# Layer 1's query panels: made ahead of the attention jobs, or beside them, two pairs ahead

## The chip, the cores and the metric

The kernel runs on one core of one Trainium2 chip. The metric is the time of one execution in device microseconds; what counts is the median of several runs. The engines are named as the profile names them: PE (TensorE, matrix products; PEld is its loading of weights), DVE (VectorE), ACT (ScalarE), POOL (GpSimd) and SP (SyncE, which here only issues DMAs).

## What is computed

Two layers of a diffusion backbone over 512 latent tokens and 256 context tokens, model width 1024, all in 32-bit floats. Layer 0 mixes latent attention and neighbourhood attention, layer 1 is sliding-window attention with 16 query heads over 2 key heads. Each layer ends in a SwiGLU block, and the result is a normalized latent stream. The part around the change is layer 1's attention. Cut to that part, the reference reads:

```python
def odd_mixer(a_lat, a_ctx, rows, cols, w_in, sinks, w_out, ctx_out):
    q, k, v = split(a_lat @ w_in, s)          # 16 query heads, 2 key and 2 value heads of 64
    q = axial_rope(q, rows, cols)
    k = axial_rope(k, rows, cols)
    qc, kc, vc = split(a_ctx @ w_in, n_ctx)
    o_lat, o_ctx = swa_heads(q, k, v, qc, kc, vc, sinks, ctx_out)
    return o_lat @ w_out, (o_ctx @ w_out if ctx_out else None)

# in swa_heads, for each block of 128 queries: scores on the 256 context keys and on the
# keys of its own block and the neighbours, a sink logit beside them, one softmax
    s_ctx = einsum(qg, kc) * scale
    s_lat = where(band_ok, einsum(qg, kb) * scale, NEG_INF)
    p = softmax(concatenate([sink, s_ctx, s_lat]))
    o = einsum(p[ctx part], vc) + einsum(p[lat part], vb)
```

## The kernel before

**Layout.** Activations are kept features by tokens. A model vector of 1024 features is eight tiles of 128 partitions. `A` (line 1545) is the modulated input of layer 1: eight pairs of tiles, each a high part and a low part, since a product of two 32-bit floats is made of three products (high by high, high by low, low by high: lines 317, 319 and 320). The 16 heads are worked as eight pairs, each pair 128 features.

**A query panel.** `swa_queries(p)` (lines 1581 to 1584) makes the queries of pair p. `load_w` (lines 301 to 308) loads 512 KB of weights by SP into a tile `wr`, ACT casts the high part `wh` (line 306), and DVE subtracts for the low part `wl` (line 307). There are three buffers of each. `project` (line 742) then runs eight times three products of 512 columns into one PSUM bank of the kind d, and yields after each three: eight steps. Behind the last, `rope` (line 443) turns the result: ACT copies it out (line 447), DVE shuffles (448), POOL multiplies twice and adds (450 to 452). `put_q` (line 687) writes it for the two heads: ACT casts each head's 64 rows (694) and DVE subtracts the low half (695).

**A job.** `swa_jobs` (line 1623) yields two jobs a pair, each with both heads and two blocks of 128 queries: 16 jobs. A job computes scores on PE (728 and 729: for each head and block two products over 256 context keys and two over 256 or 384 latent keys), adds masks and takes the running minimum on DVE (538), takes exponentials on ACT (534), transposes the 128 by 128 blocks of the weights on PE in groups of up to four (482; 18 blocks a job), copies each group out of PSUM on DVE or ACT (473, 474), and sums the values by them on PE (528). ACT copies the sum out (612). After a pair's second job `swa_finish` divides by the denominators (four transposes, 349, and a product on DVE, 465).

**Order.** `attend` (line 652) writes a job's scores between the transposes and the weighted sum of the job ahead of it, by a pattern of letters: f a step of the new job, b one of the old job, s a place for side work. There are four s in this stage's pattern (`PATTERN`, line 67). Side work is a queue of generators (`beside`, line 939). `step` (line 634) takes one step of the first generator in the queue, and a generator that ends runs its rest within the next call. `STEPS[2]` (line 72), put into `rate` at line 1642, says how many such steps are shared out over the four places of a job.

The program's text is not the final order. The tile framework traces it, gives each instruction a priority by its place in the text, and a scheduler then fixes each engine's order by priority among what is ready in a simulated timeline (`SCHED`, line 63). Larger numbers are later. `shifted` (line 627) adds to the priority of what is traced in it, and `lower[0]` is what `step` adds to side work: 150 by default (`LOWER`), 50 (`LQ`) for the query panels here. Each engine then executes its list strictly in order.

**The stage.** After the keys, the values and panel 0 (lines 1586 to 1607), panels 1 to 7 are put into side work and drained (lines 1633 to 1640), all before the first job is traced. Then come the jobs. During them the only side work is one `swa_finish` a pair, one step. After the jobs the residual `H`, which was parked in DRAM, is loaded back (1645 to 1649), the outputs are split into high and low (1650; 343, 344), and the output projection runs with `w_out1` (1652; the residual is added at 1238).

**Buffers.** The tag b has 24 tiles: `A` takes 16 until its last product; values, `k32`, `v32`, each rope's x, y and result, each pair's output, and later the residual take the others. The tag st has 12: four for the keys, two for each pair's queries, later the outputs' high parts. PSUM has eight banks: three of kind s (scores), two t, two d, one o. The groups of transposes alternate between t and d (`TURN`, line 64); the query panels take d (`PQ`, line 327).

Of the kernel before, what the change touches and what calls it, by code (L numbers as in the profile page):

```python
# [30 lines left out]
LATS = slice(0, NL)  # L31
# [14 lines left out]
LAG = 1  # L46
EV = "dr"
QF = 0
LQ, EACH = 50, 0
NR = "nb"  # L50
PE_MODS = ((0, 1), (0, 0), (0, 5))
KEEP = 1
# [12 lines left out]
LOWER = 150  # L65
# [3 lines left out]
LATE = ((0, 1, 3, 5, 7), ()), (0,) * 4 + (1, 2, 2, 2, 1, 2, 2, 2, 1, 2, 3, 2, 1, 2, 3, 2, 0, 0), ((2,), (2,)) + ((0, 2, 4, 6),) * 3  # L69
FIRST = 2000  # L70
SUMS = 5, 6
STEPS = ((2, 3, 4, 4), 5, 3)
HALVES = (slice(0, 256), slice(256, 512))
SWAP8 = [(i // 16) * 16 + (i % 16 + 8) % 16 for i in range(32)]
SWAP16 = [(i + 16) % 32 for i in range(32)]
# [23 lines left out]
def hybrid_kernel(ctx: ExitStack, tc, I, out):  # L99
# [6 lines left out]
    def T(tag, shape, dt=F32):  # L106
        count[0] += 1
        if tag not in SIZES:
            return sb.tile(shape, dt, tag=tag, name=f"{tag}_{count[0]}", bufs=BUFS.get(tag, 1))
        n = int(np.prod(shape[1:]))  # L110
        t = sb.tile([P, SIZES[tag] // (2 if dt == mybir.dt.bfloat16 else 4)], dt, tag=tag, name=f"{tag}_{count[0]}",
                    bufs=BUFS[tag])[: shape[0], :n]
        if len(shape) == 3:
            t = t.rearrange("p (a b) -> p a b", a=shape[1])
        return t

    def B(dt=F32, tag="b"):
        return T(tag, [P, NT], dt)
# [12 lines left out]
    V, S, G, PE = nc.vector, nc.scalar, nc.gpsimd, nc.tensor  # L131
# [4 lines left out]
    def f(ap):  # L136
        return ap.bitcast(F32) if ap.dtype == F32R else ap
# [3 lines left out]
    def behind(ins, *before):  # L141

        for x in before:
            tc.add_manual_dep(ins.ins, x.ins.name, mybir.DependencyInfo(mybir.DependencyClass.NoSync,
                              mybir.DependencyReason.DATA), reason="products in one run")
        return ins
# [479 lines left out]
    @contextmanager  # L626
    def shifted(by):
        tc.cur_priority += by
        yield
        tc.cur_priority -= by  # L630

    side_work, lower = deque(), [LOWER]

    def step(n=1):

        for _ in range(n):
            while side_work:
                try:
                    with shifted(lower[0]):
                        next(side_work[0])  # L640
                    break
                except StopIteration:
                    side_work.popleft()

    def drain(gen=None):

        while side_work and (gen is None or gen in side_work):
            step()
# [32 lines left out]
    def new_q(tag="st"):  # L681
        return [B(F32R, tag) for _ in range(2)]

    def new_k(tag="st"):
        return [(B(F32R, tag), B(F32R, tag)) for _ in range(2)]

    def put_q(ts, scale, hi=None, lo=None, after=()):


        def use(src, c):  # L690
            for side, t in enumerate(ts):
                r, x = slice(64 * side, 64 * side + 64), slice(64 - 64 * side, 128 - 64 * side)
                if scale is None:
                    behind((hi or S.copy)(t[r, c], src[r]), *after)
                    (lo or G.tensor_tensor)(t[x, c], src[r], f(t[r, c]), op=ALU.subtract)
                    continue
                S.activation(t[r, c], src[r], AF.Copy, scale=scale)
                V.scalar_tensor_tensor(t[x, c], src[r], scale, f(t[r, c]), op0=ALU.mult, op1=ALU.subtract)

        return use  # L700
# [24 lines left out]
    def stacked_scores(t1, ks):  # L725
        def scores(o, q, keys):
            x = t1[:, q * P : (q + 1) * P]
            PE.matmul(o, x, ks[0][:, keys], start=True, stop=False)
            PE.matmul(o, x, ks[1][:, keys], start=False, stop=True)

        return scores
# [10 lines left out]
    def project(src, use, cols=(LATS, CTXS), m=P, every=2, eng=None, w=None, get=PQ):  # L742

        w = w or load_w(src, KT, m, eng)
        for c in cols:
            o, _ = banks([c], get, m)[0]
            for k in range(KT):
                mm3([(o, c)], (w[0][:, k : k + 1], w[1][:, k : k + 1]), A[k : k + 1], k == 0, k == KT - 1)
                if k % every == every - 1:
                    yield  # L750
            use(o, c)
# [184 lines left out]
    sets = [(new_q(), new_k()) for _ in range(2)]  # L936
    for t in range(6):
        started[:] = put_vs(VN, t, ov[t])
    def beside(gen):
        side_work.append(gen)  # L940
        return gen
# [11 lines left out]
    def put_rope(t, tabs, swap, rows=P, scale=1.0, tag="b", eng=None):  # L953
        def use(src, c):
            if c is LATS:
                rope(t[:rows, c], src, tabs, swap, scale, tag, eng)
            else:
                S.activation(t[:rows, c], src, AF.Copy, scale=scale)

        return use  # L960
# [68 lines left out]
    def split_pair(p):  # L1029

        tag = ("b", "st")[p - 2]
        q, k = raws[2 * p - 4 : 2 * p - 2]
        sets.append((new_q(tag), new_k(tag)))
        up, dn = slice(0, 64), slice(64, 128)
        t0, t1 = sets[p][0]
        S.copy(t0[:, :NT], q)
        lo = q.bitcast(F32R)
        V.tensor_tensor(lo, q, f(t0[:, :NT]), op=ALU.subtract)
        yield
        dma(t1[up, :NT], t0[dn, :NT])  # L1040
        dma(t1[dn, :NT], lo[dn])
        dma(t0[dn, :NT], lo[up])
        (h0, l0), (h1, l1) = sets[p][1]
        S.copy(h0[:, :NT], k)
        V.tensor_tensor(l0[:, :NT], k, f(h0[:, :NT]), op=ALU.subtract)
        yield
        for x, y in ((h0, h1), (l0, l1)):
            dma(y[up, :NT], x[dn, :NT])
            dma(y[dn, :NT], x[dn, :NT])
            dma(x[dn, :NT], x[up, :NT])  # L1050
        yield
# [63 lines left out]
    def latent_operands(h):  # L1115
        p, s = divmod(h, 2)
        r, u = NOPE[s], USED[s]
        rr = slice(32 * (h % 4), 32 * (h % 4) + 32)
        if p < 2:
            if p == 0:  # L1120
                KA.append([T("st", [P, NT], F32R) for _ in range(2)])
            QA[s].append([T("st", [P, NT], F32R) for _ in range(2)])
            for t in [*(KA[s] if p == 0 else ()), *QA[s][p]] if s else ():
                (V if "z" in EV else G).memset(f(t[:32]), 0.0)
            if p == 0:
                for i in range(2):
                    dma(KA[s][i][ROPE[s]], KR[i][:32])
        (ka, kc), (qa, qb) = KA[s], QA[s][p % 2]
        for x, (hi, lo) in ((kn[p], (ka, kc)), (qn[p], (qa, qb))):
            S.copy(hi[r], x[r])  # L1130
            (V if "l" in EV and p < 1 else G).tensor_tensor(lo[r], x[r], f(hi[r]), op=ALU.subtract)
        for t, x in zip((qa, qb), QR[h // 4]):
            if "d" in EV:
                dma(t[ROPE[s]], x[rr])
            else:
                G.dma_start(t[ROPE[s]], x[rr])

        def scores(o, q, keys):
            q = slice(q * P, (q + 1) * P)
            PE.matmul(o, qa[u, q], ka[u, keys], start=True, stop=False)  # L1140
            PE.matmul(o, qb[u, q], ka[u, keys], start=False, stop=False)
            PE.matmul(o, qa[u, q], kc[u, keys], start=False, stop=True)

        return scores
# [12 lines left out]
    def na_jobs():  # L1157
        for p in range(4):
            if p == 3:
                lower[0] = L3  # L1160
            for x in ORDER[p]:
                beside(split_pair(int(x)) if x in "23" else {"n": latent_norms, "m": mla_prepare}[x]())
            rate[0] = STEPS[0][p], BG[p]
            if p % 2 == 0:
# [33 lines left out]
    def mla_jobs():  # L1198
        phase[0], lower[0] = 1, LOWER
        rate[0] = STEPS[1], BG[4]  # L1200
        ready.append(latent_operands(1))
# [342 lines left out]
    new = []  # L1544
# [34 lines left out]
    sets = {}  # L1579

    def swa_queries(p, every=1, get=PQ):
        q, sets[p] = B(), new_q()
        yield from project(I["w_in1"][p], put_rope(q, rope1, SWAP16, scale=0.125), (LATS,), every=every, get=get)
        put_q(sets[p], None, lo=V.tensor_tensor)(q[:, LATS], LATS)

    k32, v32, KS = B(), B(), new_k()
    kv_use = put_rope(k32, rope1, SWAP16), put(v32)
# [34 lines left out]

    def swa_jobs():
        for p in range(8):
            kv = p // 4
            po = B()
            sums, mins = T("sm", [P, 6, 2]), T("sm", [P, 6, 2])
            hs = [Head(s, stacked_scores(sets[p][s], KS[kv]), keys_of(VS, kv), span, swa_bias,
                       sink_neg[:, 2 * p + s : 2 * p + s + 1], sums, mins) for s in range(2)]
            yield from pair_jobs(hs, po, False, swa_finish(p, po, sums, mins))  # L1630
            OS.append(po)

    phase[0] = 2
    lower[0] = LQ
    for p in range(1, 8):
        beside(swa_queries(p))
        if EACH:
            drain()
            lower[0] += EACH
    drain()  # L1640
    lower[0] = LOWER
    rate[0] = STEPS[2], 0
    attend(swa_jobs())
    drain()
    H = []
# [184 lines left out]
```

## Time and profile before

| what | us |
|---|---|
| runs before, median of 3 | 1558.71 |
| lowest and highest of the 3 | 1557.58, 1560.64 |
| the profiled execution, its time | 1558.19 |
| the profiled execution, its span from first to last instruction | 1556.3 |

The page of the profile shows one execution. Busy times are sums for each engine; an instruction's row has its line, its engine, its output and inputs by the program's names (buffer numbers left out: `psd` is any bank of kind d), its shape and count. A number in brackets or behind a bar is idle time of the engine just before, with what ended it. A matmul's length is modelled and overlaps the next one, so what PE has to spend on one is read from the distance between two starts. The chain of the profile is followed back from the last instruction, at each step to what released it; its rows have a start and the time that counted. The windows give busy times between two moments, counted from the start of the span.

### The profile page before, as it was taken

Reading aid. Unit: us, or ns where it says so; the run is one execution under the profiler, and the core shown is the slowest. Engines: PE = TensorE matmul, PEld = TensorE weight load, DVE = VectorE, ACT = ScalarE, POOL = GpSimd, SP = SyncE. Lnnn points to the kernel's source line nnn. Section 1 sums busy time; section 2 is a strip of 40 time slices with the busy share of each in tenths; the row PEclk is TensorE's granted clock in tenths of the full one; section 3 lists DMA queues with packets and bytes.
Section 4 is the critical chain, followed back from the end, with each engine's and each line's share of the span. In section 5 each row is a group of like instructions: output and inputs, shape, how many; then the busy total and the mean of one; then the engine's idle time right before and its main releaser. Section 6 shows DMA issues by size and latency. Waiting matters only on the chain.

```text
span 1556.3 us, 26589 instructions
## 1 busy us (share of the span) xinstructions
PE 1529.0 (98%) x10048; PEld 1374.9 (88%) x10048; DVE 1176.5 (76%) x2408; ACT 768.0 (49%) x1531; POOL 217.0 (14%) x269
## 2 busy tenths in 40 slices
PE   9999999999999999999999999999999999999998
PEld 8788877877999898999999988877789899899998
DVE  4799867676868687777768676789967779678685
ACT  4532677674555242432424335457856455354453
POOL 0021043110101102012021122470012000000001
PEclk9999999999999999999999999999999999999999
DMA  9674632013634545537465494110214223323222
GB/s 321 249 226 142 161 125 65 11 63 138 227 128 139 206 134 182 205 118 288 142 249 187 150 358 139 55 41 1 90 57 167 63 91 126 107 84 131 88 94 89
DMA packets 79073, 219.39 MB, mean 141 GB/s; under 512 B 10720, under 2 KB 17888, under 8 KB 78944
## 3 DMA queue, kind: packets, MB, share of 16 engines
q1 hardware_dynamic: 61280, 147.42, 28.6%
q0 software_dynamic: 16512, 68.69, 12.4%
q8 instruction: 79, 1.29, 0.3%
q10 hardware_dynamic: 1152, 1.57, 0.3%
q14 instruction: 50, 0.41, 0.1%
HBM read 186.97 MB, written 23.07 MB: 135 GB/s over the span
## 4 chain that ended last, share of the span: by engine, by line
PE 88%; DVE 7%; ACT 2%; issue 2%; DMA 1%; POOL 0%; DVEq 0%; ACTq 0%; POOLq 0%
PE pss L1401 5%; PE pss L1400 5%; PE pss L1399 5%; PE pso L528 5%; PE pss L320 4%; PE pss L317 4%; PE pss L319 4%; PE psd L317 4%; PE psd L320 4%; PE psd L319 4%; PE pst L317 3%; PE pst L320 3%; PE pst L319 3%; PE pst L1401 3%; PE pst L1399 3%; PE pst L1400 3%
## 5 line engine op out<-in xcount | busy, mean ns | idle before, releaser
L306 ACT CAST wh<-wr 128x1024 fp32r<-128x1024 f32 (+2 forms) x148 | 115.5, 795 | 224.2 <-DMA wr<-in_w_dn_dram 35.0
L307 DVE TENSOR_TENSOR wl<-wr,wh 128x1024 fp32r<-128x1024 f32 (+2 forms) x145 | 130.9, 910 | 80.6 <-ACT wh L306 76.3
L534 ACT ACTIVATE p<-p,sm 128x512 f32<-128x512 f32 (+3 forms) x144 | 105.0, 730 | 25.8 <-DVE sm L538 25.2
L1399 PE MATMUL pss<-b,wh 128*128 128x384 f32 (+1 forms) x346 | 107.7, 312 | 0.5 <-ACT b L343 0.5
L1400 PE MATMUL pss<-b,wh 128*128 128x384 f32 (+1 forms) x346 | 107.8, 312 | 0.0
L1401 PE MATMUL pss<-b,wl 128*128 128x384 f32 (+1 forms) x346 | 107.0, 311 | 0.0
L319 PE MATMUL psd<-b,wh 128*128 128x512 f32 (+2 forms) x254 | 88.6, 349 | 0.0
L273 DVE CUSTOM_DVE_ANT_0 p<-rope,cond 128x1024 bf16<-128x1024 f32 x64 | 76.8, 1219 | 11.4 <-DMA rope<-in_mod_w_dram 11.2
L317 PE MATMUL psd<-b,wh 128*128 128x512 f32 (+2 forms) x214 | 79.1, 370 | 2.8 <-ACT pl L474 2.2
L528 PE MATMUL pso<-ph,b 128*64 128x256 f32 (+1 forms) x384 | 77.9, 362 | 1.0 <-DVE ph L473 0.9
L528 PE MATMUL pso<-pl,b 128*64 128x256 f32 (+1 forms) x384 | 78.4, 363 | 0.0
L320 PE MATMUL psd<-b,wl 128*128 128x512 f32 (+2 forms) x214 | 77.5, 363 | 0.0
L1401 PE MATMUL pst<-b,wl 128*128 128x384 f32 (+1 forms) x226 | 70.6, 313 | 1.5 <-DVE wl L1387 1.5
L1386 ACT CAST wh<-pl 128x512 fp32r<-128x512 f32 x78 | 44.9, 619 | 53.6 <-PE pss L1400 22.7
L1399 PE MATMUL pst<-b,wh 128*128 128x384 f32 (+1 forms) x226 | 70.7, 313 | 0.6 <-ACT p L1449 0.6
L263 POOL DMA_DIRECT2D rope<-in_mod_w_dram x48 | 25.6, 533 | 323.0 <-DVE mod L273 312.1
L1400 PE MATMUL pst<-b,wh 128*128 128x384 f32 (+1 forms) x226 | 70.5, 312 | 0.0
L1386 ACT CAST wh<-wr 128x1024 fp32r<-128x1024 f32 x39 | 41.0, 1051 | 57.7 <-PE pst L1400 14.8
L319 PE MATMUL pss<-b,wh 128*128 128x256 f32 (+3 forms) x216 | 68.4, 316 | 0.0
L317 PE MATMUL pss<-st,wh 128*128 128x512 f32 (+2 forms) x198 | 67.5, 341 | 0.3 <-ACT wh L306 0.3
L320 PE MATMUL pss<-st,wl 128*128 128x512 f32 (+2 forms) x198 | 67.5, 341 | 0.1
L1399 PEld LDWEIGHTS pss<-b,wh 128*128 128x128 f32 x346 | 65.0, 188 | 1.1 <-ACT b L343 0.8
(606 smaller groups left out, 5290.7 us busy)
## 6 DMA issues: line engine op xcount, KB each, us to landing
wr<-in_w_gu_dram SPq DMA_DIRECT2D x88, 512.0 KB, 4.1
rope<-in_mod_w_dram POOLq DMA_DIRECT2D x48, 512.0 KB, 3.9
wr<-in_w_dn_dram SPq DMA_DIRECT2D x73, 256.0 KB, 2.9
wr<-in_w_out_dram SPq DMA_DIRECT2D x32, 512.0 KB, 3.9
p<-home POOLq DMA_DIRECT2D x40, 384.0 KB, 5.6
home<-p POOLq DMA_DIRECT2D x40, 384.0 KB, 5.9
wr<-in_w_in_dram SPq DMA_DIRECT2D x21, 512.0 KB, 3.9
ph<-in_mod_w_dram SPq DMA_DIRECT2D x24, 256.0 KB, 2.8
```

What stands on the lines that cost most here:

```text
L273: behind(V.tensor_tensor_reduce(out=T("p", [P, D], mybir.dt.bfloat16), in0=w, in1=cond[:, v, :], op0=ALU.mult, op1=ALU.add, scale=1.0, sca ...
L306: behind(S.copy(h, r), *after[:1])
L307: behind((G if eng else V).tensor_tensor(lo, r, f(h), op=ALU.subtract), *after[1:])
L317: ins = PE.matmul(o, wh[:, k], mh[:, c], start=first and k == 0, stop=False)
L319: PE.matmul(o, wh[:, k], ml[:, c], start=False, stop=False)
L320: PE.matmul(o, wl[:, k], mh[:, c], start=False, stop=last and k == n - 1)
L528: ins = PE.matmul(o[64 * i : 64 * i + 64, c], v(kt), t, start=n == 0, stop=n == len(moving[i]) - 1)
L534: S.activation(p[:, c], p[:, c], AF.Exp, bias=nm, scale=-1.0, accum_out=dn)
L1386: S.copy(h, t)
L1399: PE.matmul(o, wh, xh, start=first and k == 0, stop=False, skip_group_check=not first)
L1400: PE.matmul(o, wh, xl, start=False, stop=False, skip_group_check=not first)
L1401: PE.matmul(o, wl, xh, start=False, stop=k == 3, skip_group_check=not first)
```

## The change

Panels 2 to 7 are no longer drained ahead of the jobs. Panel 1 alone is. At the beginning of pair p, for p below 6, the generator of panel p + 2 is put into the side work, and it is stepped at the places of the jobs, with five steps a job instead of three and the default of 150 added to the priority in place of 50. A pair's two jobs thus have ten steps, for the eight of a panel, in whose wake the rope and `put_q` are traced, and the one of the finish. `sets[p]` is now set when a panel is complete, and a pair whose panel is not complete steps the side work until it is.

```diff
@@ -46,7 +46,6 @@
 LAG = 1
 EV = "dr"
 QF = 0
-LQ, EACH = 50, 0
 NR = "nb"
 PE_MODS = ((0, 1), (0, 0), (0, 5))
 KEEP = 1
@@ -69,7 +68,7 @@
 FIRST = 2000
 SUMS = 5, 6
-STEPS = ((2, 3, 4, 4), 5, 3)
+STEPS = ((2, 3, 4, 4), 5, 5)
 HALVES = (slice(0, 256), slice(256, 512))
@@ -1579,9 +1578,10 @@
     sets = {}
 
     def swa_queries(p, every=1, get=PQ):
-        q, sets[p] = B(), new_q()
+        q, new = B(), new_q()
         yield from project(I["w_in1"][p], put_rope(q, rope1, SWAP16, scale=0.125), (LATS,), every=every, get=get)
-        put_q(sets[p], None, lo=V.tensor_tensor)(q[:, LATS], LATS)
+        put_q(new, None, lo=V.tensor_tensor)(q[:, LATS], LATS)
+        sets[p] = new
 
@@ -1622,6 +1622,10 @@
 
     def swa_jobs():
         for p in range(8):
+            while p not in sets:
+                step()
+            if p < 6:
+                beside(swa_queries(p + 2))
             kv = p // 4
             po = B()
             sums, mins = T("sm", [P, 6, 2]), T("sm", [P, 6, 2])
@@ -1631,14 +1635,8 @@
             OS.append(po)
 
     phase[0] = 2
-    lower[0] = LQ
-    for p in range(1, 8):
-        beside(swa_queries(p))
-        if EACH:
-            drain()
-            lower[0] += EACH
+    beside(swa_queries(1))
     drain()
-    lower[0] = LOWER
     rate[0] = STEPS[2], 0
     attend(swa_jobs())
     drain()
```

## The prediction

> **What bounds the kernel now.** I read the page first, then the stretch of layer 1's queries and attention by windows, then its PE timeline, its chain, its waits and its groups. The page says that there is little to win anywhere on PE:
>
> ```profile
> span 1556.3 us, 26589 instructions
> PE 1529.0 (98%) x10048; PEld 1374.9 (88%) x10048; DVE 1176.5 (76%) x2408; ACT 768.0 (49%) x1531; POOL 217.0 (14%) x269
> ```
>
> The change touches one stretch. The windows below (us, then busy time of PE, PEld, DVE, ACT, POOL, granted clock, DMA) split it where the first weighted sum of the attention (L528) starts:
>
> ```profile
> 985.00:1042.70 57.70, 56.16 (x291) 46.62 (x289) 46.84 (x83) 31.56 (x53) 45.59 (x29) 1.00 0.21 64
> 1042.70:1147.00 104.30, 102.83 (x840) 81.98 (x839) 95.06 (x315) 80.59 (x196) 0.00 (x0) 1.00 0.10 37
> ```
>
> Before 1042.7 PE makes all query panels while POOL turns them (45.6 us busy). After it PE and DVE are both nearly full and POOL does nothing. PE at 102.8 of 104.3 is a modelled figure, so I check it by starts. Rows of the PE timeline (start, us, what) give what one matmul takes from PE when PE is fed:
>
> ```profile
> 1011.30 0.28 PE L728 MATMUL pss<-st,st 128*128 128x256 f32 x1
> 1011.42 0.28 PE L729 MATMUL pss<-st,st 128*128 128x256 f32 x1
> 1011.78 0.39 PE L317 MATMUL psd<-b,wh 128*128 128x512 f32 x1
> ...
> 1017.14 0.39 PE L320 MATMUL psd<-b,wl 128*128 128x512 f32 x1
> 1017.37 0.28 PE L728 MATMUL pss<-st,st 128*128 128x256 f32 x1
> ...
> 1017.61 0.34 PE L728 MATMUL pss<-st,st 128*128 128x384 f32 x1
> 1017.79 0.33 PE L729 MATMUL pss<-st,st 128*128 128x384 f32 x1
> ...
> 1018.44 0.50 PE L317 MATMUL psd<-b,wh 128*128 128x512 f32 x1 [0.32 <-ACT b L447]
> ```
>
> A panel is the 24 matmuls from 1011.78 to 1017.37: 5.6 us, 0.233 each. A score matmul takes 0.12 (256 columns) or 0.18 (384). The chain has four transposes in 0.44 us and a job's weighted sum in 2.10:
>
> ```profile
> 1036.33 0.44 PE psd L482 x4
> ...
> 1042.79 2.10 PE pso L528 x20
> ...
> 1144.87 2.17 PE pso L528 x20
> ```
>
> The first and last of the 16 weighted sums start 102.08 us apart, so 15 jobs take 6.81 us each. What a job needs of PE: scores of two heads and two query blocks, 12 x 0.1175 + 4 x 0.176 = 2.11; 18 transposes x 0.11 = 1.98; the weighted sum 2.10; two transposes of the finish (four a pair) 0.22; going into and out of the weighted sum about 0.2 (an estimate from the starts around it: 0.21 instead of 0.12 from the last score to the first L528, and as much again behind it). Together 6.6. So a job leaves PE idle for **about 0.2 us**, 3 us over 16 jobs. Two single holes come on top, at the end of the panels, and the 0.32 above; and that PE turned to the weighted sum is seen in the last two rows:
>
> ```profile
> 1040.59 0.33 PE L482 MATMUL pst<-ident_r,p 128*128 128x128 f32 x1 [0.34 <-ACT p L534]
> ...
> 1042.06 0.39 PE L728 MATMUL pss<-st,st 128*128 128x256 f32 x1 [0.81 <-DVE sm L538]
> ...
> 1042.51 0.28 PE L729 MATMUL pss<-st,st 128*128 128x256 f32 x1
> 1042.72 0.43 PE L528 MATMUL pso<-pl,b 128*64 128x256 f32 x1
> ```
>
> That is all that can be won: 3.0 + 1.15 + 0.32, about **4.5 us or 0.3%**. What keeps PE waiting is the path through DVE and ACT, by the waits of 1040 to 1147:
>
> ```profile
> ACT p L534 <- DVE sm L538: 11.7, 16, 3.3
> DVE p L538 <- PE pss L729: 4.2, 4, 1.4
> ```
>
> **The change part by part.** No instruction is added or removed; panels 2 to 7 move. A panel's cost on each engine, by the groups between 985 and 1145 (mean ns of one after the comma):
>
> ```profile
> L306 ACT CAST wh<-wr 128x1024 fp32r<-128x1024 f32 x10 | 10.4, 1044 | 3.1 <-PE pst L319 3.0
> L447 ACT ACTIVATE b<-psd 128x512 f32<-128x512 f32 x8 | 4.7, 591 | 7.4 <-PE psd L320 5.1 <-DVE b L448 2.4
> L694 ACT CAST st<-b 64x512 fp32r<-64x512 f32 x16 | 9.9, 617 | 10.6 <-POOL b L452 7.2 <-PE pss L729 3.2
> L307 DVE TENSOR_TENSOR wl<-wr,wh 128x1024 fp32r<-128x1024 f32 x10 | 13.0, 1313 | 0.2 <-ACT wh L306 0.2
> L448 DVE STREAM_SHUFFLE b<-b 128x512 f32<-128x512 f32 x9 | 6.7, 742 | 0.0
> L450 POOL TENSOR_TENSOR b<-b,rope 128x512 f32<-128x512 f32 x9 | 13.2, 1462 | 24.0 <-DVE b L448 24.0
> L451 POOL TENSOR_TENSOR b<-b,rope 128x512 f32<-128x512 f32 x9 | 13.9, 1544 | 0.0
> L452 POOL TENSOR_TENSOR b<-b,b 128x512 f32<-128x512 f32 x9 | 15.2, 1686 | 0.7
> ```
>
> ACT: 1.04 + 0.59 + 2 x 0.62 = 2.9 us. POOL: 4.7 us. DVE: 1.3 + 0.74 and two low halves (L695):
>
> ```profile
> L695 DVE TENSOR_TENSOR st<-b,st 64x512 fp32r<-64x512 f32 x6 | 8.5, 1419 | 1.5 <-ACT st L694 1.4
> L538 DVE CUSTOM_DVE_ANT_0 p<-pss,zeros,sink_neg 128x256 f32<-128x256 f32 x6 | 2.7, 482 | 4.7 <-PE pss L729 4.6
> ...
> L538 DVE CUSTOM_DVE_ANT_0 p<-pss,zeros,sink_neg 128x256 f32<-128x256 f32 x56 | 24.6, 475 | 1.2 <-PE pss L729 1.1
> L695 DVE TENSOR_TENSOR st<-b,st 64x512 fp32r<-64x512 f32 x6 | 4.1, 686 | 0.2
> ```
>
> The first two rows are from 1005 to 1040, with POOL busy, the last two from 1045 to 1145, with POOL idle. The low half takes twice as long beside POOL; the attention's own DVE work (L538, fed from PSUM) does not mind. So moving POOL's work among the jobs should not slow them: 3.4 to 4.9 us of DVE a panel. [...]
>
> *PE.* A panel beside a pair's two jobs adds 2.8 us to each: 9.4 us, of which DVE then needs its present 6.8 x 95.06/104.3 = 6.2 plus 2.5 at most, and ACT 6.8 x 80.59/104.3 = 5.3 plus 1.4. PE is the bound there with 0.7 us to spare on DVE, so nearly all 0.2 us holes of these jobs can be filled. Six panels last 12 jobs at most; as five steps a job give ten a pair and a panel with a finish needs nine, I count 11 jobs: 11 x 0.2 = 2.2 us. The holes at 1018.4 and 1040.6 to 1042.1 go too, since the next panel's matmuls can stand there: 1.15 + 0.32. **Gain, 3.7 us.** The last jobs have no panel left and keep 6.8. The jobs start earlier, but PE's total, 5.6 us a panel, is the same, so nothing else follows from that.
>
> *Start.* Only panel 1 is drained ahead of the jobs. The first score waits for the keys, and PE has to be fed until then:
>
> ```profile
> 1004.64 0.57 PE L728 MATMUL pss<-st,st 128*128 128x256 f32 x3
> ```
>
> Panel 2's weights wait for nothing but buffers, and the scheduler may pull it forward as it pulled scores between panels at 1011.30. I take nothing; the price if it does not is one panel, 5.6 us.
>
> *Queues.* SP's loads of the panels' weights spread out; they were done by 1006, and what else stands on that queue is far ahead of its use (SP's timeline, and the first use of the reloaded residual on DVE's):
>
> ```profile
> 991.15 14.88 SPq L134 DMA_DIRECT2D wr<-in_w_in_dram  x4
> 1011.59 13.28 SPq L134 DMA_DIRECT2D wr<-in_w_out_dram  x3
> ```
>
> ```profile
> 1120.77 4.00 SPq L134 DMA_DIRECT2D b<-parked  x8
> ```
>
> ```profile
> 1154.84 0.48 DVE L1238 SCALAR_TENSOR_TENSOR b<-psd,mod,b 128x256 f32<-128x256 f32 x1 [3.84 <-PE psd L320]
> ```
>
> The eight reloads of the residual need b buffers, which the normalized input (16 of the 24) now keeps until panel 7. Panel 7 is due in pair 5, about three quarters through the stretch, near 1110, so they can still go at 1120. Cost nothing; the cover is the 34 us until 1154.8. With 16 tiles of the input, the values and up to five outputs in b, a panel's three rope tiles may have to wait for panel 7's first products; that pulls panel 7 forward and costs no PE time.
>
> *The new wait.* ACT takes the turned panel from POOL (L694, then L695), and whatever stands behind that on ACT waits. Here is what it did between 990 and 1040:
>
> ```profile
> ACT st L694 <- POOL b L452: 7.2, 2, 6.0
> ```
>
> It cost nothing there because PE had panels queued. Among the jobs the exponentials (L534) stand behind it, and behind them transposes and weighted sum. Spread over eight panels this is 0.9 us each; the ends are 0 and the 6.0 of the longest. ACT is idle for 23% of the jobs' time and PE has panel products between, so I charge about half of 0.9 to PE: 6 x 0.45 = 2.7.
>
> **Sum:** -3.7 + 2.7 = -1.0 us, against the profiled execution's 1558.2 (span 1556.3 and 1.9 around it): 1557.2. The median shown is 1558.7, 0.5 above it; I say **1557.5**. A measurement of this kernel can tell about 0.2%, 3.1 us.
>
> **The rivals.**
> *Everything is filled and ACT never waits long.* For: PE is the bound in the mixed jobs, and what stalls it is DVE and ACT, which gain slack there. Against: orders are fixed ahead, and the waits above show that real durations miss them. Gain 3.7 to 4.5: 1554.2 to 1555.0, say 1554.7. [...]
> *Slower: ACT behind POOL.* If the full 0.9 us a panel, and not the half, reaches PE through L534, and nothing is won: 6 x 0.9 = 5.4, 1564; with part of the gain 1562.5. It decides once more than 0.6 us a panel (3.7/6) reaches PE.
> *Slower: one bank fewer.* A panel holds one of the two d banks for more than a job, so every second group of transposes has a single bank, and waits for its copy:
>
> ```profile
> L473 DVE COPY pl<-psd 128x512 f32<-128x512 f32 x15 | 10.0, 683 | 0.4 <-PE psd L482 0.4
> ```
>
> Once a job for 12 jobs, 12 x 0.68 = 8 us: 1566. Against: the groups then come 1.9 us apart, and PE has panel products to do meanwhile.
> *The order hardly changes.* The scheduler may pull the panels forward to where they are now, as it moves output weights from far behind to 1011. Then 1558.7.
>
> **How the numbers follow.** Forecast 0.37, order unchanged 0.10, all filled 0.27, ACT behind POOL 0.19, bank 0.07. Faster is the third, 0.27; slower the last two, 0.26; within 0.2% the rest, 0.47. The range runs from the full gain with a little more (4.5 and the last job's holes, 1553.5) to the priced wait (1564).
>
> **What would show it.** Panel evictions (L447) among the jobs to about 1110; the first weighted sum near 1020 instead of 1042.8; starts of weighted sums 9 to 9.5 us apart while panels last, 6.8 after; the last one near 1144. The slower case shows as ACT L534 or L694 waiting for POOL among the jobs and PE waiting for L534; the bank case as L482 waiting for L473 or L474. I am wrong if the stretch needs more than three us less or more than it did.

## The result and the profile after

The changed kernel is slower. Its median is 1566.50 us (six runs, 1564.92 to 1569.81), that of the kernel before beside it 1558.14 (six runs, 1555.32 to 1560.64); the ratio is 1.0048, with a 95% interval of 1.0034 to 1.0061. (It compares the runs of one set with each other and is not the quotient of the two medians; so it is in the table further down.) Of the runs further down two slow executions, one of the run called twice (8539 us) and one of the kernel before (1864 us), are left out. The prediction was 1557.5 with a range of 1553.5 to 1564.0: wrong, and with the wrong sign.

Up to line 1580 the changed kernel's lines are one lower than before: the weighted sum is L527, scores L727 and L728, transposes L481, the minimum L537, the exponential L533, the weights' low half L306, the rope's end on POOL L451, `put_q` L693 and L694. The page of the profiled execution (1566.58 us):

```profile
span 1564.8 us, 26579 instructions
PE 1531.7 (98%) x10048; PEld 1377.1 (88%) x10048; DVE 1176.2 (75%) x2408; ACT 768.7 (49%) x1531; POOL 214.2 (14%) x269
```

The sums say nothing: the busy times are nearly those of before, only the span is 8.5 us longer. The stretch does. First and last weighted sum in PE's timeline:

```profile
1024.98 0.43 PE L527 MATMUL pso<-pl,b 128*64 128x256 f32 x1
...
1152.86 0.43 PE L527 MATMUL pso<-ph,b 128*64 128x256 f32 x1 [0.21 <-DVE ph L472]
```

The first comes 17.7 us earlier (1042.72 before), the last 8.0 later (1144.87). The windows on both sides of the first, columns as before:

```profile
985.00:1024.98 39.98, 32.49 (x174) 27.88 (x172) 36.06 (x71) 24.91 (x44) 23.52 (x14) 0.83 0.18 66
1024.98:1152.86 127.88, 125.89 (x936) 101.55 (x935) 102.64 (x323) 86.84 (x205) 19.03 (x15) 1.00 0.12 38
```

The second window is in order: PE is busy for 125.9 of 127.9 us at full clock. The first is not: 7.5 us without PE, and a granted clock of 0.83. Five-microsecond windows of it, of the kernel before and then of the changed one:

```profile
1005.00:1010.00 5.00, 5.00 (x26) 4.18 (x25) 4.92 (x8) 1.74 (x3) 3.50 (x2) 1.00 0.36 107
1010.00:1015.00 5.00, 5.00 (x25) 4.13 (x24) 4.76 (x10) 2.20 (x3) 4.40 (x4) 1.00 0.39 105
1015.00:1020.00 5.00, 4.68 (x22) 3.59 (x22) 4.71 (x10) 4.94 (x10) 2.97 (x3) 1.00 0.00 0
```

```profile
1005.00:1010.00 5.00, 0.52 (x4) 0.28 (x3) 4.92 (x10) 1.30 (x2) 3.91 (x3) 0.79 0.28 107
1010.00:1015.00 5.00, 2.61 (x8) 1.76 (x8) 4.94 (x13) 2.78 (x4) 4.44 (x3) 0.50 0.26 105
1015.00:1020.00 5.00, 4.40 (x20) 4.40 (x21) 4.88 (x14) 4.14 (x11) 2.24 (x2) 0.50 0.00 0
```

DVE (third busy time) is as full in both. What differs is PE: before, panels 3 to 7 run there; after, there is next to nothing. The scheduler did pull panel 2 forward, both kernels have panels 1 and 2 behind them at 1005, but panel 3 is traced only with pair 1. PE's timeline of the changed kernel:

```profile
1004.81 0.58 PE L728 MATMUL pss<-st,st 128*128 128x256 f32 x3
1009.87 0.55 PE L727 MATMUL pss<-st,st 128*128 128x256 f32 x1 [4.48 <-DVE sm L537]
1010.22 0.41 PE L728 MATMUL pss<-st,st 128*128 128x256 f32 x1
1010.43 0.41 PE L727 MATMUL pss<-st,st 128*128 128x256 f32 x1
...
1011.46 0.58 PE L727 MATMUL pss<-st,st 128*128 128x256 f32 x1 [0.40 <-DVE sm L537]
...
1015.60 0.47 PE L481 MATMUL psd<-ident_r,p 128*128 128x128 f32 x1 [2.59 <-ACT p L533]
```

The first scores fill their banks; then PE waits 4.48 us for DVE's minima to free one, and 2.59 us for the first exponential. After the first pause the products are slow: at a granted clock of 0.50 two score products of 256 columns start 0.21 us apart, against 0.1175 in the prediction. DVE's timeline shows what stands ahead of the minima:

```profile
1002.00 1.96 DVE L714 TENSOR_TENSOR st<-b,st 64x768 fp32r<-64x768 f32 x1
1003.99 1.23 DVE L306 TENSOR_TENSOR wl<-wr,wh 128x1024 fp32r<-128x1024 f32 x1
1005.14 0.01 DVE L447 LOAD_MASK_SELECT b<-b  x1
1005.14 0.72 DVE L447 STREAM_SHUFFLE b<-b 128x512 f32<-128x512 f32 x1
1005.90 0.95 DVE L708 TENSOR_TENSOR st<-b,st 64x768 fp32r<-64x768 f32 x1
1006.87 1.92 DVE L714 TENSOR_TENSOR st<-b,st 64x768 fp32r<-64x768 f32 x1
1008.82 0.48 DVE L537 CUSTOM_DVE_ANT_0 p<-pss,zeros,sink_neg 128x256 f32<-128x256 f32 x1
...
1009.64 1.36 DVE L306 TENSOR_TENSOR wl<-wr,wh 128x1024 fp32r<-128x1024 f32 x1
...
1013.41 2.76 DVE L694 TENSOR_TENSOR st<-b,st 64x512 fp32r<-64x512 f32 x2
```

DVE hardly pauses. Between job 0's first scores and its first minimum stand a shuffle and the keys of the second key head (L708 and L714: 0.95 + 1.92 us, needed from pair 4 on); among the minima stand the low weights of one panel (L306 at 1009.64), another shuffle and the writing of panel 1's queries. On ACT the exponential stands behind the same panel 1. ACT's timeline, of the changed kernel and then of the one before:

```profile
1012.16 1.26 ACT L693 CAST st<-b 64x512 fp32r<-64x512 f32 x2 [5.86 <-POOL b L451]
1013.44 1.28 ACT L533 ACT_TABLE_LOAD   x1
1014.73 0.72 ACT L533 ACTIVATE p<-p,sm 128x512 f32<-128x512 f32 x1
```

```profile
1012.75 1.26 ACT L694 CAST st<-b 64x512 fp32r<-64x512 f32 x2 [5.99 <-POOL b L452]
```

The same wait, at the same time, stood in the kernel before. PE had panels to make there meanwhile, and was busy in all of 1005 to 1015.

**A sum for all runs.** Each product of a stretch is counted at the spacing that it has when PE is fed (0.233 us for 512 columns, 0.176 for 384, 0.1175 for 256, 0.11 a transpose, 2.10 + 0.2 a weighted sum); what is left is idle PE. From 985 to the first weighted sum this gives 3.0 us idle before and 13.2 after (**+10.2**); from there to the end of the last one 5.7 before and 4.0 after (**-1.7**). The net of 8.5 us is what the span grew by. What a halved clock adds to a product counts as idle in this sum. Of the 13.2 us, 7.5 are pauses of PE, and at most 4.4 come from the half clock (the products from 1009.87 to 1021.55 add up to 4.4 us at full speed). The profiled executions reach this stage up to 8 us apart, so the runs below are also compared by the time from the stage's first product over the context columns (before L317 at 986.89, after L316 at 986.42) to the first and to the last weighted sum: 55.8 and 158.0 us before, 38.6 and 166.4 after. The second is called the stretch.

### The profile page after: what moved, and what is told of

Same layout as the page of the kernel before. It is cut to its first block, busy times and chain, and to the rows that moved or that the text cites. A ratio compares the mean times of both kernels' runs of the same rounds, so it can differ in the third digit from the quotient of the medians.

```text
span 1564.8 us, 26579 instructions
## 1 busy us (share of the span) xinstructions
PE 1531.7 (98%) x10048; PEld 1377.1 (88%) x10048; DVE 1176.2 (75%) x2408; ACT 768.7 (49%) x1531; POOL 214.2 (14%) x269
## 4 chain that ended last, share of the span: by engine, by line
PE 85%; DVE 6%; DMA 4%; ACT 3%; issue 1%; POOL 0%; SPq 0%; DVEq 0%; ACTq 0%; POOLq 0%
PE pso L527 5%; PE pss L1400 5%; PE pss L1399 5%; PE pss L1398 5%; PE psd L316 4%; PE psd L318 4%; PE psd L319 4%; PE pss L319 4%; PE pss L316 4%; PE pss L318 4%; PE pst L316 3%; PE pst L319 3%; PE pst L318 3%; PE pst L1400 3%; PE pst L1398 3%; PE pst L1399 3%
## 5 line engine op out<-in xcount | busy, mean ns | idle before, releaser
L306 DVE TENSOR_TENSOR wl<-wr,wh 128x1024 fp32r<-128x1024 f32 (+2 forms) x145 | 131.4, 913 | 80.8 <-ACT wh L305 76.3
L533 ACT ACTIVATE p<-p,sm 128x512 f32<-128x512 f32 (+3 forms) x144 | 105.0, 731 | 35.8 <-DVE sm L537 35.3
L316 PE MATMUL psd<-b,wh 128*128 128x512 f32 (+2 forms) x214 | 79.6, 372 | 1.9 <-ACT pl L473 1.6
L527 PE MATMUL pso<-ph,b 128*64 128x256 f32 (+1 forms) x384 | 78.6, 364 | 0.9 <-DVE ph L472 0.9
L527 PE MATMUL pso<-pl,b 128*64 128x256 f32 (+1 forms) x384 | 78.3, 363 | 0.7 <-ACT pl L473 0.6
L316 PE MATMUL pss<-st,wh 128*128 128x512 f32 (+2 forms) x198 | 67.7, 342 | 0.4 <-ACT wh L305 0.4
L727 PE MATMUL pss<-st,st 128*128 128x256 f32 (+3 forms) x194 | 61.1, 338 | 5.0 <-DVE sm L537 4.9
```

Of the source, the lines that this page charges most:

```text
L306: behind((G if eng else V).tensor_tensor(lo, r, f(h), op=ALU.subtract), *after[1:])
L316: ins = PE.matmul(o, wh[:, k], mh[:, c], start=first and k == 0, stop=False)
L527: ins = PE.matmul(o[64 * i : 64 * i + 64, c], v(kt), t, start=n == 0, stop=n == len(moving[i]) - 1)
L533: S.activation(p[:, c], p[:, c], AF.Exp, bias=nm, scale=-1.0, accum_out=dn)
```

## The experiments

The theory after the result: job 0's start is bound by DVE and by ACT behind POOL, and needs the panels as PE's cover. Its rivals: that the half clock is the cause, that one more panel ahead would do, and that the panels cost something among the jobs. "Changed" is the changed kernel, "stretch" the difference to the 158.0 us of before in the profiled execution; idle is PE's by the sum above, ahead of the first weighted sum and behind it (among the jobs). The last four columns are of one profiled execution each. Runs are compared by their ratios, since each set has its own runs of the kernel before.

| run | median us (its before) | ratio, 95% interval | first weighted sum after the stage's first product | idle ahead of it | idle among the jobs | stretch |
|---|---|---|---|---|---|---|
| before | 1558.14 | | 55.8 | 3.0 | 5.7 | 0 |
| changed | 1566.50 (1558.14) | 1.0048 (1.0034 to 1.0061) | 38.6 | 13.2 | 4.0 | +8.5 |
| two_ahead | 1567.69 (1558.81) | 1.0056 (1.0042 to 1.0070) | 41.0 | 12.0 | 7.2 | +10.4 |
| three_ahead50 | 1568.39 (1558.81) | 1.0052 (1.0035 to 1.0070) | 45.9 | 8.2 | 8.0 | +7.4 |
| five_ahead | 1561.66 (1559.36) | 1.0016 (1.0005 to 1.0027) | 54.0 | 4.2 | 7.6 | +3.0 |
| five3 | 1559.66 (1558.49) | 1.0011 (1.0002 to 1.0019) | 53.8 | 3.9 | 5.6 | +0.9 |
| seven_ahead | 1559.90 (1558.49) | 1.0010 (1.0000 to 1.0020) | 55.9 | 3.0 | 6.8 | +1.1 |
| seven_keys | 1561.70 (1559.36) | 1.0018 (1.0007 to 1.0028) | 55.4 | 2.7 | 9.1 | +2.9 |
| seven3_keys | 1558.07 (1558.49) | 0.9997 (0.9986 to 1.0007) | 55.4 | 2.6 | 5.8 | -0.4 |
| twice | 1568.26 (1558.81) | 1.0052 (1.0037 to 1.0066) | 37.6 | 7.6 | 3.6 | +8.2 |
| late_put | 1564.59 (1558.81) | 1.0033 (1.0019 to 1.0048) | 36.4 | 11.7 | 3.9 | +6.7 |
| late_keys | 1564.24 (1559.36) | 1.0044 (1.0028 to 1.0061) | 36.2 | 11.4 | 4.0 | +6.6 |
| late_both | 1564.84 (1559.36) | 1.0044 (1.0030 to 1.0058) | 34.5 | 9.3 | 5.4 | +5.8 |
| both_far | 1566.98 (1558.49) | 1.0049 (1.0036 to 1.0062) | 32.2 | 7.1 | 9.0 | +7.3 |

### More panels ahead: two, three

```diff
-            if p < 6:
-                beside(swa_queries(p + 2))
+            if p < 5:
+                beside(swa_queries(p + 3))
...
-    beside(swa_queries(1))
+    for p in (1, 2):
+        beside(swa_queries(p))
     drain()
```

Three ahead likewise, with `p < 4`, `p + 4` and 50 added to the priority while they drain.

> Panels 1 and 2 are drained ahead of the jobs, and panel p + 3 goes beside pair p (the changed kernel drains panel 1 alone and has p + 2 there). Theory, a hole at the start: behind panel 2 PE has nothing to do until job 0's exponentials come (some 9 us of idle time and 3 us of halved clock), while the jobs themselves gain about 2 us. One more panel, 5.6 us, then fills half of the hole: some 5 to 7 us less than the changed kernel, 1559 to 1562, first weighted sum near 1026 to 1028. Rival, the jobs beside panels are slow (POOL's result holds up ACT, one bank less): the time stays within 2 us of the changed kernel.

> Panels 1 to 3 are drained ahead with 50 added to the priority, and panel p + 4 goes beside pair p. By the hole at the start, two further panels (11.2 us) fill all of it: the clock stays at 1.00 from 1000 to 1030 and the time is 8 to 10 us below the changed kernel, 1556 to 1558, thus level with the kernel before or up to 2 us below it. By the rival it stays within 3 us of the changed kernel, as three or four panels still go beside jobs.

Both theories miss: neither gains, though PE has 24 and 48 products of 512 columns more (5.6 and 11.2 us) ahead of the first weighted sum. The times are those of the rivals, but hardly for their reason: among the jobs ACT waits for POOL 0.3 and 0.2 us in all, PE for the copies of transposes 1.0 and 1.4. Each panel brings its weights, shuffle and low halves to DVE, ahead of or among job 0's minima, so the first weighted sum moves back too, by 2.4 and 7.3 us. With three ahead PE idles 5.0 us less at the start and 4.0 more among the jobs; why so much more there was not followed. With two ahead the hole at the start hardly shrinks, as PE's timeline shows:

```profile
1014.36 0.47 PE L481 MATMUL psd<-ident_r,p 128*128 128x128 f32 x1 [2.99 <-ACT p L533]
...
1025.15 0.69 PE L727 MATMUL pss<-st,st 128*128 128x384 f32 x1 [3.33 <-DVE sm L537]
```

Both stand ahead of the first weighted sum (1026.08). Between the first and the second another 2.1 us count as idle, nearly all of it half clock: the granted clock is 0.50 from about 1023.6 to 1030.4 (by windows of 2 us), and the first weighted sum takes 4.04 us there instead of 2.10. The theory that one more panel would fill the start falls.

### Work for PE alone: panel 1's products made twice

```diff
+            if extra:
+                o, _ = banks([c], get, m)[0]
+                for k in range(KT):
+                    mm3([(o, c)], (w[0][:, k : k + 1], w[1][:, k : k + 1]), A[k : k + 1], k == 0, k == KT - 1)
...
-        yield from project(I["w_in1"][p], put_rope(q, rope1, SWAP16, scale=0.125), (LATS,), every=every, get=get)
+        yield from project(I["w_in1"][p], put_rope(q, rope1, SWAP16, scale=0.125), (LATS,), every=every, get=get, extra=p == 1)
```

> The changed kernel with the 24 products of panel 1 done a second time into a bank that nobody reads: 5.6 us more work for PE. By the hole at the start this work stands where PE would have idled and keeps the clock up: no more than 1 us over the changed kernel, and up to 3 us below it. By the rival, with PE the bound all along, it adds 5.6 us.

PE does 5.6 us more, DVE and ACT nothing more. The median stands 1.8 us above the changed kernel's, but the two ratios, 1.0052 and 1.0048, cannot be told apart; in the profiled execution the stretch even is 0.3 us shorter, and the idle time falls by 5.6, from 13.2 to 7.6. So PE's hole is real and takes PE work at little or no cost.

### Less for DVE and ACT at the start: the queries, the keys, both

```diff
         if p == 1:
+            late.append(lambda: put_q(new, None, lo=V.tensor_tensor, after=(marks["exp"],))(q[:, LATS], LATS))
...
-    put_k(KS, KC[2])(k32, slice(0, NT))
+    put_k(KS[:1], KC[2])(k32, slice(0, NT))
+    late.append(lambda: put_k(KS[1:], KC[2], first=1)(k32, slice(0, NT)))
...
-            yield from pair_jobs(hs, po, False, swa_finish(p, po, sums, mins))
+            for j in pair_jobs(hs, po, False, swa_finish(p, po, sums, mins)):
+                yield j
+                while late:
+                    late.pop()()
```

The first hunk is late_put, the second late_keys; late_both has both, and the third belongs to each. What is in `late` is traced behind job 0's scores.

> The changed kernel with the two casts and low halves of panel 1 traced after job 0's scores and put behind its exponentials on ACT. If the hole is made by ACT standing 5.9 us before POOL's result with the exponentials behind it, ACT gets to them at about 1012 instead of 1014.7 and the first weighted sum comes 2 to 3 us earlier; 2 to 3 us less time. If DVE's list (the low halves of the keys, then the scores' minimum) sets it, less than 1 us.

> The changed kernel, with the keys of the second key head (needed from pair 4 on) written after job 0's scores instead of before them: some 2.9 us of DVE and 1.4 us of ACT leave the start. Theory (the start is bound by DVE's panel and key work together with ACT's wait for POOL): the first weighted sum comes 2 to 3 us earlier than 1024.98, near 1022, and the time is 1563.5 to 1565. Rival (ACT's wait for POOL alone sets the start): the first weighted sum stays within 0.7 of 1024.98 and the time at 1566 to 1567.

> The keys of the second head and the writing of panel 1's queries both behind job 0's scores. Theory: the two savings add up, so the first weighted sum is 6 to 7 us earlier than 1024.98, near 1018.5, PE idles 8 to 9 us ahead of it instead of 13.2, and the time is 1561.5 to 1563. Rival (the two lie on the same wait): as with the queries alone, 1020.8 and 1564.6.

Each alone brings the first weighted sum 2.2 and 2.4 us forward when counted from the stage's first product, both together 4.0: the shares add nearly, though by its raw start (1021.13) the last run looked like no gain over the first (1020.77), whose execution had come to the stage 2.2 us earlier. So job 0's weighted sum hangs on DVE's and ACT's lists; which of the two counts more is open, since each run takes work off both (late_put also moves the 2.76 us of low halves on DVE). By time the three cannot be told from the changed kernel: the intervals of their ratios overlap its own. The median of late_put is 1.9 us lower, that of late_keys lies where the theory put it, and that of late_both (1564.84) missed its 1561.5 to 1563 and is the rival's 1564.6; late_both idles 1.4 us more among the jobs. The loss does not need the half clock. These are late_keys' windows, and the longest wait that its PE timeline shows there:

```profile
1005.00:1010.00 5.00, 2.75 (x16) 2.14 (x17) 5.00 (x16) 2.71 (x6) 4.82 (x4) 1.00 0.61 166
1010.00:1015.00 5.00, 2.99 (x22) 2.28 (x19) 4.91 (x12) 4.93 (x9) 4.08 (x3) 1.00 0.11 43
1015.00:1020.00 5.00, 2.80 (x17) 1.83 (x16) 4.86 (x13) 2.95 (x7) 0.00 (x0) 1.00 0.00 0
```

```profile
1005.89 0.35 PE L727 MATMUL pss<-st,st 128*128 128x256 f32 x1 [1.39 <-DVE sm L537]
```

The clock stays at 1.00, PE is fed in small portions and idles 11.4 us all the same, with DVE full; the stretch is still 6.6 us longer than before.

### The keys out of the start altogether

The same as late_both, with the keys written when two pairs are done (`len(OS) == 2`). In late_both they had stayed ahead of the first weighted sum, by DVE's timeline:

```profile
1017.55 0.95 DVE L708 TENSOR_TENSOR st<-b,st 64x768 fp32r<-64x768 f32 x1
1018.52 0.95 DVE L714 TENSOR_TENSOR st<-b,st 64x768 fp32r<-64x768 f32 x1
```

> The changed kernel with panel 1's queries written behind job 0's scores, and the keys of the second head written only in pair 2, so that their 1.9 us on DVE are not among job 0's minima any more, as they still were with both behind job 0's scores. Theory (DVE's list up to job 0's last copy sets the first weighted sum): it comes 1 to 2 us earlier than 1021.1, 1019 to 1020, and the time is 1562.5 to 1564. Rival (another chain of 1021 stands behind it): 1021 and 1564.8.

The start does as expected: the first weighted sum comes at 1019.74, another 2.4 us earlier from the stage's first product, with 7.1 us idle ahead of it. The time does not: 1566.98. The jobs idle 9.0 us in this execution (4.0 in the changed kernel), 4.0 of it between the weighted sums at 1108.79 and 1120.09, where the panels end. ACT's timeline there:

```profile
1110.47 0.83 ACT L533 ACTIVATE p<-p,sm 128x640 f32<-128x640 f32 x1 [1.02 <-DVE sm L537]
...
1111.55 1.26 ACT L693 CAST st<-b 64x512 fp32r<-64x512 f32 x2
1112.84 1.14 ACT L342 CAST st<-b 128x512 fp32r<-128x512 f32 x2
1113.88 0.47 ACT L473 COPY ph<-pst 128x384 f32<-128x384 f32 x1
1114.25 1.13 ACT L342 CAST st<-b 128x512 fp32r<-128x512 f32 x2
1115.29 0.72 ACT L533 ACTIVATE p<-p,sm 128x512 f32<-128x512 f32 x1
```

The exponential at 1115.29 stands behind two casts of the last panel and four of finished outputs, with no panel left to cover it. The products are slow there too: on PE those from 1116.37 on take 3.72 us until the weighted sum at 1120.09, against 1.92 at the spacings of the sum above (score products of 256 columns start 0.21 us apart), which can account for up to 1.8 of the 4.0 us. What the late keys cost here was not tried alone.

### Five ahead, and the steps by themselves

```diff
-            if p < 6:
-                beside(swa_queries(p + 2))
+            if p < 2:
+                beside(swa_queries(p + 6))
...
-    beside(swa_queries(1))
+    lower[0] = 50
+    for p in range(1, 6):
+        beside(swa_queries(p))
     drain()
+    lower[0] = LOWER
```

seven_ahead has `range(1, 8)` and none beside: the kernel before with five steps a job. five3 and seven3_keys have `STEPS[2]` at 3; seven_keys and seven3_keys write the second head's keys late, the one behind job 0's scores, the other in pair 2.

> Panels 1 to 5 drained ahead of the jobs as in the kernel before (50 added), panels 6 and 7 alone beside jobs. Theory (a panel that is missing from the cover of the start costs about 1.5 us there, and a panel beside a pair of jobs wins about 0.4): PE idles 5 to 6 us ahead of the first weighted sum (3.0 before, 8.2 with three panels ahead), the time is 1 to 2 us above the kernel before, 1560 to 1561. Rival (the loss comes with the work beside the jobs, in proportion to the panels there): two of six panels, 8.4 x 2/6 = 2.8 above, with the idle at the start as before.

> All seven panels drained ahead as in the kernel before (five steps a job stay), and the keys of the second head written after job 0's scores. Theory: DVE's load at the start still costs the kernel before a part of its 3.0 us of idle PE ahead of the first weighted sum; with 2.9 us of DVE gone that falls to 1 to 2 us and the time to 1557 to 1558.5, beside 1559. Rival (with seven panels as cover the start is hidden entirely, and the 3.0 us are of another cause): 1559 within 0.5.

> The kernel before with one thing of the change alone: five steps of side work a job instead of three; all seven panels stay ahead of the jobs, so the steps only move each pair's finish. Theory (with the panels gone from the side work, five steps put the finish at a worse place): the start is as before (about 3.0 us idle ahead of the first weighted sum near 1042.7), the jobs idle about 9 us instead of 5.7, 1561 to 1562. Rival (steps that have nothing to take cost nothing, and the run with the late keys was slower by its keys): 1559 within 0.5.

> The kernel before with the keys of the second head written in pair 2 and nothing else changed (three steps). Theory (the start of the kernel before is covered by the panels on PE, and the five steps cost what the run before lost): 1558 to 1559.5, the same as before. Rival (writing the keys late among the jobs costs DVE time there): 1561 to 1562.

> Panels 1 to 5 ahead, 6 and 7 beside the jobs, but with three steps a job. Theory: the start idles about 4.2 us as with five steps (1.2 more than before), the jobs idle what they do in the kernel before less about 0.8 for the two panels, so 1559 to 1560. Rival (the panels beside the jobs cost by themselves): 1561 to 1562, as with five steps.

five_ahead and seven_keys came out 2.3 us above the kernel before. five_ahead idles 4.2 us at the start, between the theory's 5 to 6 and the rival's 3.0; seven_keys lies above both its theories. The last three runs explain them in part: with all panels ahead, five steps by themselves give 1.0010 (stretch +1.1, idle among the jobs 6.8 us instead of 5.7, start unchanged), about half of what was expected and hardly above the error. That leaves 1.8 us of the stretch of seven_keys to the keys behind job 0's scores, which was not followed further. With three steps, five panels ahead and two beside give 1.0011: 1 us lost at the start and nothing gained behind it. Three steps with panels two pairs ahead were not tried. The late keys, with three steps, change nothing (0.9997): with seven panels as cover, the start's load on DVE is hidden. No version here is measurably better than the kernel before; what it has left to win is 8.7 us of idle PE, and each way tried to win some of it lost as much at the start or among the jobs.

## Why the prediction was wrong, step by step

- **The bound** (PE) is right, and it is why a missing cover costs at once. The cap of 4.5 us was about half of it: idle by the sum above is 3.0 + 5.7. (In the forecast itself 1557.2 and 0.5 make 1557.7, not 1557.5; nothing hangs on that.)
- **PE's gain, 11 jobs x 0.2 = 2.2:** right in size. Idle among the jobs fell by 1.7; beside the kernel with five steps alone, 6.8 to 4.0, by 2.8. With panels in them, the jobs are nearly without holes (PE busy 125.9 of 127.9). The weighted sums come 9.5 us apart on average over the first ten gaps and 6.6 over the last five, much as foretold.
- **The holes of 0.32 and 1.15** did not go. They sat in job 0's start, which the change opened.
- **"Start: I take nothing; the price if it does not is one panel, 5.6 us"** is the step that failed, a term of the sum mis-sized: 0 charged, 10.2 us measured. What was asked of the trace was right (panel 2 was pulled forward), but the question was too small. PE had to be fed not until the first scores at 1004.6, but until the first weighted sum, through DVE's minima, ACT's wait for POOL and the table load (1.28 us). Before, panels 3 to 7, 28 us of PE, stood there. The row for ACT's 6.0 us was quoted, with the words that it cost nothing because PE had panels queued; that the change takes these very panels away was not drawn from it.
- **Queues:** nothing lost. From the last weighted sum to the span's end there are 411.9 us after and 411.4 before.
- **The new wait, 2.7 us among the jobs,** did not come. From 1025 to 1153 no wait of ACT for POOL is on record. These rows of the waits there are the nearest to it and to the bank rival:

```profile
ACT p L533 <- DVE sm L537: 21.6, 20, 2.5
...
PE pst L481 <- ACT ph L473: 0.6, 1, 0.6
...
PE pst L481 <- DVE ph L472: 0.3, 1, 0.3
```

- **The rivals.** The slower one named a wait that counts, in the wrong place: ACT behind POOL stood at the start, once, and not six times among the jobs. Putting its casts and DVE's low halves later (late_put) brought 2.2 us there; its share alone is not shown. The bank rival (8 us at L481) has 0.9. "Order unchanged" is out: the last of the panels is turned near 1114, by the groups from 1025 to 1114:

```profile
L447 DVE STREAM_SHUFFLE b<-b 128x512 f32<-128x512 f32 x5 | 3.7, 749 | 0.0
```

Five panels, as foretold for the time to about 1110. The first weighted sum near 1020 was foretold as well and came at 1024.98; it looks like an advantage, and only the PE work that lies ahead of it tells that it is not: 54.7 us of work in 57.7 before, 26.8 in 40.0 after.

What the sum should have been: +10.2 at the start, -1.7 among the jobs.

## What to carry to other kernels

Before work is moved away from a place, ask what it covers there, and follow the chain of the next stage to its first steady point (here the first weighted sum), not to its first instruction. Here, work that filled PE at a stage's start was worth more than the same work in small holes of the steady state (10.2 us against 1.7); and one or two panels more covered less than their own 5.6 and 11.2 us (1.2 and 5.0 of the idle time), as they also brought load to DVE, on which the start hung.

## What the runs showed of the hardware

- The granted clock fell to 0.50 at 1007.90 in the changed kernel, 2.5 us after the last score product had ended (1005.39) and within the pause of 4.48 us, and it came back at 1021.55, though PE had worked without a break since 1015.60. It fell without a long pause too: in both_far between 1010 and 1015 (0.66 in that window) with no pause above 1.40 us, in late_both between 1020 and 1025 (0.66) with none above 1.6, while in late_keys, with none above 1.39, it stayed at 1.00. These are both_far's window and the longest pause ahead of its fall:

```profile
1010.00:1015.00 5.00, 4.96 (x25) 4.67 (x26) 5.00 (x19) 4.23 (x10) 4.84 (x5) 0.66 0.36 105
```

```profile
1007.95 0.35 PE L727 MATMUL pss<-st,st 128*128 128x256 f32 x1 [1.40 <-DVE sm L537]
```

- The half clock lasts 13.65 us in the changed kernel (1007.90 to 1021.55), four times the 3.41 us that it lasts from 963.53 to 966.94 in the same execution; by the windows it lasts about 6.8 us in late_put and twice, about 3.4 in late_both and both_far. In the changed kernel it ended with the fourth 3.41 us (1018.14 to 1021.55), the first of the four that PE filled: PE was busy for 1.19, 1.55 and 2.54 us of the three before. In the 3.41 us ahead of the fall PE had 0.65 us of work by the sum above. PE's busy time in windows of 5 us does not tell a fall: it was 2.27 us in both_far (1005 to 1010) and 2.40 in late_both (1015 to 1020), each just ahead of the window with the fall, but 2.25 in late_both from 1005 to 1010 too, and the clock stayed at 1.00 until 1020; late_keys has 2.75 or more in each window from 1005 to 1030. What sets the fall and the return was not shown.
- The low half of a head's queries (L694) took 1.38 us each while POOL worked (2.76 for two at 1013.41) and 0.69 at 1020.37, where it was idle; the keys' L714 took 1.92 us in the changed kernel (at 1006.87, POOL at work) against 0.95 in late_both (at 1018.52, POOL idle): the slowing beside POOL named in the prediction, here in the way of job 0. Not every such row is slower: the keys' L708 took 0.95 us in both, though in the changed kernel (at 1005.90) POOL was at work from 1006.01 on.
